# Modulation chunks mixed into the weight streams in pairs, and two of layer 1's modulation rounds moved later

## Chip, core and metric

One NeuronCore of a Trainium2 chip runs the whole kernel. The metric is the device time of one execution in microseconds. Of the kernel before, three executions were timed: 2155.64, 2166.26 and 2171.59 us, median 2166.26 us.

## What is computed

Two transformer layers run over 256 latent tokens and 256 context tokens, 1024 features wide, in float32:

```python
for l in range(DEPTH):                                   # 2 layers
    mod_l = cond_lat @ ada_w[l] + ada_b[l]               # 6 rows of 1024 from silu(c)
    mod_c = cond_ctx @ ada_w[l] + ada_b[l]
    sh1, sc1, g1, sh2, sc2, g2 = jnp.split(mod_l, 6, axis=-1)
    ...
    o_lat, o_ctx = token_mixer(modulate(x, sh1, sc1), modulate(xc, csh1, csc1), lp, rope, need_ctx)
    x = post_norm(alpha * x + g1 * o_lat, ln1_g[l], ln1_b[l])
    ...
    f_lat = swiglu(modulate(x, sh2, sc2), ...)           # layer 0; layer 1: moe_swiglu, top 2 of 8 experts
    x = post_norm(alpha * x + g2 * f_lat, ln2_g[l], ln2_b[l])
```

`token_mixer` is attention, an RWKV-7 scan and a Hyena convolution side by side, then one output projection. Layer 0 does all of it for both streams; in layer 1 the context is only read by the latent tokens.

The change concerns the modulation, `cond @ ada_w[l]`. A round makes two of the six rows: round 0 makes sh1 and sc1, round 1 g1 and sh2, round 2 sc2 and g2. So the first norm of a layer needs round 0, the residual norm after the mixer needs g1 of round 1, and the channel mixer needs rounds 1 and 2.

## The kernel before

All weights come from HBM in chunks of 512 KB ([128, 1024] float32), most of them issued on SP's DMA queue (tile `wraw`). `wload` loads a chunk and splits it into a rounded part and a rest: a cast on ScalarE (`whi`, L315) and a subtraction on VectorE (`wlo`, L316). Every product is then three passes on TensorE (`mm3`, L321 to L323). The number of buffers for raw chunks and for split pairs goes by the stage, `BUFS`: 6 raw and 4 pairs in stage "l" (both streams of layer 0, layer 1's context), 5 and 4 in stage "n" (layer 1's latent tokens), 30 and 4 in stage "m" (the experts).

The modulation is not split. `ada` (a generator) loads one chunk of `adaw` into a raw buffer of the stage's own ring and multiplies it as it is, in four matmuls that use a quarter of the array's columns each (tile `ada`, L392; the trace has two records for each of the four). Sixteen chunks make a round. After the last one VectorE adds the bias (L397), for rounds 1 and 2 two small stores put the rows into DRAM (`drow`), four transposes (`adaT`, L404) and copies put them feature-major into `modT`. The rows that are needed on all partitions are read back from `drow` by `modbc` (L420): `gate` in `post_norm`, `m_sc`, `m_sh` and `gate` in `moe_route`.

A generator in `s.fill` is mixed into the weight stream: each `wload` runs one step of it, which is one chunk of modulation:

```python
        if s.fill:
            next(s.fill, None)
```

Layer 0's rounds 1 and 2 are mixed into its first two mixers this way. All three rounds of layer 1 (48 chunks) are mixed into layer 0's channel mixer of the context, whose 66 weight chunks are products `ab` (L321 to L323, 24 matmuls with 256 columns to a chunk) and `fo` (12 matmuls with 512 columns).

After that come layer 0's channel mixer of the latent tokens, layer 1's context, and layer 1's latent part: `win` (input projection, tile `u`), `rwkv`, `attend` (`aS`, `aPT`, `ao`), the last four Hyena tiles of `win`, `hyena` (`Xc`, `Xs`, `hz`, `ho`) and `w_out` (tile `wo`, eight weight chunks), with its residual norm on VectorE (`pnr`, `x`). `moe_route` then picks the experts, and `moe_pass` streams 528 chunks of expert weights.

The program's order is not the order on an engine: the framework places instructions of independent parts between each other on each engine's queue. The queues are then run strictly in that order, and each instruction waits for what it needs.

Of the kernel before, what the change touches and what calls it, by code (L numbers as in the profile page):

```python
# [5 lines left out]
D = 1024  # L6
L = 256
# [8 lines left out]
def feature_tiles():  # L16
    """Columns of w_in per 128-wide tile, -1 for padding."""
    t = []
# [44 lines left out]
NLAST = 512  # of the first group, kept throughout  # L63
# [8 lines left out]
def constants():  # L72
# [11 lines left out]
    # x -> (-x1, x0) on pairs: out[m] = sum_k perm[k, m] x[k]  # L84
# [14 lines left out]
    ang = np.concatenate([row[:, None] * inv, col[:, None] * inv], -1).astype(np.float64)  # [L, 32]  # L99
# [6 lines left out]
    S = np.sin(th)  # [t, k]  # L106
    S[:, 0] = (-1.0) ** k  # column k = 0 holds the Nyquist term
    put("C", C.reshape(2, 128, 256).transpose(1, 0, 2))
    # forward: lhsT [t, k]; inverse: lhsT [k, t] -> S transposed
# [17 lines left out]
    a, b = (p % 32)[:, None], np.arange(32)[None]  # row s, column t  # L127
    # per direction: (A, B, -A, B) masks; A strict, B inclusive
# [3 lines left out]
    # token order: ltri[p, tt, q] = 1 where token tt*128+p precedes q within the tile  # L132
# [5 lines left out]
    # within a chunk, from its first (second) half to the other one  # L138
# [5 lines left out]
def layout(i):  # L144
    """Device arrays from the inputs: layout only."""
    g = lambda n: np.asarray(i[n])
    A = {}
# [7 lines left out]
    aw = g("ada_w").reshape(2, 8, 128, 3, 4, 2, 256)  # l, k, p, r, j, h, n  # L155
    A["adaw"] = np.ascontiguousarray(aw.transpose(0, 3, 5, 1, 2, 4, 6))  # l, r, h, k, p, j, n
# [12 lines left out]
    A["win"] = np.ascontiguousarray(wp.reshape(2, 8, 128, 20, 128).transpose(0, 3, 2, 1, 4))  # l, tile, p, k, 128  # L169
    wo = g("w_out")[:, mix_rows()]  # L170
    A["wout"] = np.ascontiguousarray(wo.reshape(2, 4, 2, 128, 2, 512).transpose(0, 4, 1, 3, 2, 5))  # l, half, kh, p, k, n

    def w13(w1, w3):  # [..., 1024, 2816] -> [..., 11, kh, p, k, (w1 256 | w3 256)]
        e = w1.shape[0]
        u = np.stack([w1, w3], 1).reshape(e, 2, 4, 2, 128, 11, 256)  # e, m, kh, k, p, b, n
        return np.ascontiguousarray(u.transpose(0, 5, 2, 4, 3, 1, 6)).reshape(e, 11, 4, 128, 2, 512)

    def w2(w):  # [e, 2816, 1024] -> [e, half, 22, p, 512]
        e = w.shape[0]
        u = w.reshape(e, 11, 2, 128, 2, 512)  # L180
        return np.ascontiguousarray(u.transpose(0, 4, 1, 3, 2, 5))  # e, half, 11, p, 2, 512
# [6 lines left out]
    A["rows"] = np.stack([g("ln1_g"), g("ln1_b"), g("ln2_g"), g("ln2_b")], 1)  # l, 4, 1024  # L188
    pr = np.zeros((2, 128, NPRM), np.float32)

    def pp(name, a, col=0, r0=0):  # a: [2, rows]
        pr[:, r0:r0 + a.shape[1], PRM[name] + col] = a

    mu = g("rwkv_mu")  # [2, 2, 864]
# [64 lines left out]
class Trunk:  # L259
# [4 lines left out]
    def lasting(s, n):  # L264
        """n words per partition that are kept throughout."""
        assert s.used + n <= NLAST + s.SMALL
        s.used += n
        return s.keep[:, s.used - n:s.used]

    def k(s, shape, name, dt=F32):  # L270
        """A tile. All of the pool's are of 4 KB per partition: up to 1 (2) KB, four (two) of a name share
        one; up to 512 bytes, the slots of a small lasting ring are used in turn."""
# [24 lines left out]
    def fresh(s, *names):  # L297
        """The next small tiles of these names do not share one with the past ones."""
# [14 lines left out]
    def split(s, src, hi, lo, eng="a"):  # L313
        """hi + lo == src; both fit a float32r pass exactly."""
# [3 lines left out]
    def mm3(s, out, a, b, start, stop, **kw):  # L318
        """out += a.T @ b from (hi, lo) pairs: three float32r passes."""
# [5 lines left out]
    def rsqrt(s, x, n, eps, name):  # L325
        """x[:, :n] -> 1 / sqrt(x + eps): an estimate from the exponent, then Newton steps to float32."""
# [10 lines left out]
    def raw(s, src):  # L337
        """The next 4 KB per partition of the weight stream."""
# [4 lines left out]
        if s.w == "m" and s.loads % 16 == 0:  # some through another queue  # L343
# [6 lines left out]
    def wload(s, src):  # L350
        """A weight chunk (4 KB per partition) as an exact (hi, lo) pair."""
# [5 lines left out]
        if s.fill:  # L357
            next(s.fill, None)
        return hi, lo

    def drain(s):
        """The rest of the loads mixed into the weight stream."""
# [4 lines left out]
    def order(s, inst, first):  # L367
        """inst is not to be issued before first."""
# [3 lines left out]
    def behind(s):  # L372
        """Loads not to be issued before the last weight load so far."""
        return s.tc.issue_after(s.last.ins) if s.last is not None else contextlib.nullcontext()

# [1 line left out]
    def ada(s, l, rounds):  # L377
        """Rounds of two of the six rows of the modulation, in steps of one weight chunk."""
# [38 lines left out]
    def modbc(s, l, st, prm, name):  # L417
        """Row prm of a stream's modulation on all partitions: a [128, 1024] tile."""
# [6 lines left out]
    def ln_stats(s, src):  # L425
        """src: list of [128, 1024] -> (mean list, rstd list)."""
# [16 lines left out]
    def hT(s, l, st, prm, src, f32=None):  # L443
        """LN(src) * (1 + scale) + shift, feature-major, split: eight (hi, lo) pairs [128, 256]."""
# [24 lines left out]
    def win_steps(s, l, tiles, g):  # L469
        """u^T tiles of w_in from g["h"], each to its consumer."""  # L470
# [14 lines left out]
    def conv3(s, u, out, cp, cc, cn, bias):  # L485
        """out[t] = cp * u[t-1] + cc * u[t] + cn * u[t+1] + bias over the 256 tokens."""
# [9 lines left out]
class Mix(Trunk):  # L496
# [1 line left out]
    def sin_of(s, ps, f, fb, out):  # L498
        """out = sin(f * ps + fb), the argument reduced to [-pi, pi]."""
# [15 lines left out]
    def spec_load(s, l):  # L515
        """Filter parameters of a layer; the larger ones by a second call."""
# [1227 lines left out]
```

## Time and profile before

| | |
|---|---|
| timed executions | 2155.64, 2166.26, 2171.59 us |
| span of the profiled execution (first to last instruction) | 2151.5 us |
| median less this span | 14.8 us |
| TensorE busy | 2061.4 us (96%) |
| VectorE busy | 1650.1 us (77%) |
| ScalarE busy | 1117.6 us (52%) |
| moved by DMA | 469.15 MB, 218 GB/s on average |

The profiled execution's own time is given by its span only; what lies around the span (launch, end) is not in the trace, so the 14.8 us hold that and the spread of the executions. A TensorE that is busy is not a TensorE at its peak, since the ends of matmuls are modelled; the starts are measured. Shares over the whole span mix stages with different limits, so the rows below are by stage. The granted clock of TensorE is 1.00 at 2.4 GHz and 0.50 at 1.2 GHz.

### The profile page before, as it was taken

To read this page: it belongs to the slowest core of one execution; us is meant where nothing else is said; L and a number is where in the kernel's file an instruction comes from. 1 tells how busy PE (TensorE), PEld (TensorE's weight loads), DVE (VectorE), ACT (ScalarE), POOL (GpSimd) and SP (SyncE) were. 2 spreads that over 40 slices of the span, in tenths; PEclk is the share of its full clock that TensorE was granted. 3 is DMA by queue.
4 is the path that set the end of the run, shared out by engine and by line. 5 is a ranking of instruction groups with operands and counts; after the bars stand their busy time and mean duration, and the time that the engine had idled before them with its cause. 6 is when DMAs were issued, how large, how long until landed. Compare 5 with 4: busy or idle time off the path is not lost. (4 is left out here: it accounts for less than half of the span.)

```text
span 2151.5 us, 35770 instructions
## 1 busy us (share of the span) xinstructions
PE 2061.4 (96%) x13674; PEld 1684.2 (78%) x13674; DVE 1650.1 (77%) x3026; ACT 1117.6 (52%) x1639; POOL 111.3 (5%) x87
## 2 busy tenths in 40 slices
PE   8999999999999999989798998999999999999996
PEld 2878777678878898887487777788888888888885
DVE  6897777459754685776887448799899989998997
ACT  3532544242332344443244232787787877778773
POOL 0012001100000000010111100000000000000000
PEclk9999999999999999999899978899999999999998
DMA  8522332336686545323211018699999999999992
GB/s 292 191 74 98 138 129 90 114 115 230 247 335 244 196 177 196 138 88 113 104 60 33 31 56 335 218 319 362 363 334 368 354 344 350 361 358 345 360 356 107
DMA packets 147852, 469.15 MB, mean 218 GB/s; under 512 B 31636, under 2 KB 33972, under 8 KB 147672
## 3 DMA queue, kind: packets, MB, share of 16 engines
q1 hardware_dynamic: 123512, 446.27, 56.8%
q0 software_dynamic: 4816, 17.36, 2.2%
q10 hardware_dynamic: 19344, 3.15, 0.8%
q8 instruction: 109, 1.79, 0.3%
q14 instruction: 71, 0.58, 0.1%
HBM read 464.56 MB, written 2.16 MB: 217 GB/s over the span
## 5 line engine op out<-in xcount | busy, mean ns | idle before, releaser
L316 DVE TENSOR_TENSOR wlo<-wraw,whi 128x1024 fp32r<-128x1024 f32 x748 | 888.0, 1222 | 96.2 <-ACT whi L315 61.7
L315 ACT CAST whi<-wraw 128x1024 fp32r<-128x1024 f32 x748 | 751.7, 1049 | 143.6 <-DMA wraw<-in_fw_dram 40.6
L321 PE MATMUL ab<-whi,m_x 128*128 128x512 f32 x704 | 281.6, 400 | 0.0
L323 PE MATMUL ab<-whi,m_x 128*128 128x512 f32 x704 | 275.6, 391 | 0.0
L322 PE MATMUL ab<-wlo,m_x 128*128 128x512 f32 x704 | 275.0, 391 | 0.0
L321 PE MATMUL ab<-hp,whi 128*128 128x256 f32 x704 | 204.8, 292 | 2.6 <-ACT hp L315 2.0
L323 PE MATMUL ab<-hp,wlo 128*128 128x256 f32 x704 | 201.7, 287 | 1.8 <-DVE wlo L316 1.8
L322 PE MATMUL ab<-hp,whi 128*128 128x256 f32 x704 | 201.7, 287 | 1.3 <-DVE hp L316 1.1
L323 PEld LDWEIGHTS ab<-whi,m_x 128*128 128x128 f32 x704 | 132.1, 188 | 28.3
L321 PE MATMUL u<-hp,whi 128*128 128x256 f32 x512 | 150.2, 297 | 4.1 <-ACT hp L315 3.0
L322 PEld LDWEIGHTS ab<-wlo,m_x 128*128 128x128 f32 x704 | 132.5, 188 | 25.5 <-DVE wlo L316 0.2
L321 PEld LDWEIGHTS ab<-whi,m_x 128*128 128x128 f32 x704 | 132.2, 188 | 25.1
L321 PEld LDWEIGHTS ab<-hp,whi 128*128 128x128 f32 x704 | 135.9, 194 | 18.3 <-issue 11.0
L323 PE MATMUL u<-hp,wlo 128*128 128x256 f32 x512 | 147.9, 291 | 1.2 <-DVE wlo L316 1.1
L322 PE MATMUL u<-hp,whi 128*128 128x256 f32 x512 | 148.1, 292 | 0.0
L323 PEld LDWEIGHTS ab<-hp,wlo 128*128 128x128 f32 x704 | 136.1, 194 | 5.3 <-DVE wlo L316 2.9
L322 PEld LDWEIGHTS ab<-hp,whi 128*128 128x128 f32 x704 | 136.5, 194 | 2.1 <-DVE hp L316 2.0
L321 PE MATMUL mo<-whi,ffg 128*128 128x512 f32 x352 | 137.8, 392 | 0.0
L323 PE MATMUL mo<-whi,ffg 128*128 128x512 f32 x352 | 137.1, 390 | 0.0
L322 PE MATMUL mo<-wlo,ffg 128*128 128x512 f32 x352 | 137.0, 389 | 0.0
L957 POOL TENSOR_TENSOR rBD<-rAT,cst 128x1024 f32<-128x1024 f32 x28 | 67.5, 2418 | 932.8 <-DVE rTm L995 509.9
L321 PEld LDWEIGHTS u<-hp,whi 128*128 128x128 f32 x512 | 98.4, 194 | 15.9 <-issue 6.5
(395 smaller groups left out, 3610.3 us busy)
## 6 DMA issues: line engine op xcount, KB each, us to landing
wraw<-in_mw_dram SPq DMA_DIRECT2D x495, 512.0 KB, 5.6
wraw<-in_fw_dram SPq DMA_DIRECT2D x132, 512.0 KB, 5.2
wraw<-in_adaw_dram SPq DMA_DIRECT2D x96, 512.0 KB, 5.1
wraw<-in_win_dram SPq DMA_DIRECT2D x64, 512.0 KB, 5.7
wraw<-in_mw_dram POOLq DMA_DIRECT2D x33, 512.0 KB, 6.8
wraw<-in_wout_dram SPq DMA_DIRECT2D x24, 512.0 KB, 3.6
lngb<-in_rows_dram SPq DMA_DIRECT2D x12, 512.0 KB, 6.3
x<-in_xs_dram SPq DMA_DIRECT2D x8, 512.0 KB, 6.0
```

Of the source, the lines that this page charges most:

```text
L315: i = (s.nc.scalar.copy if eng == "a" else s.nc.vector.tensor_copy)(hi, src)
L316: return i, s.nc.vector.tensor_sub(lo, src, hi.bitcast(F32))
L321: mm(out, a[0], b[0], start=start, stop=False, **kw)
L322: mm(out, a[0], b[1], start=False, stop=False, **kw)
L323: mm(out, a[1], b[0], start=False, stop=stop, **kw)
L957: i = nc.gpsimd.tensor_mul(x.rearrange("p u (j t) -> p u j t", j=4), bc(ATu[:, :, m, None, :], [128, 8, 4, 32]), bc(mask.rearrange("p (j t ...
```

## The change

`wload` now runs the generator at every second call only, `rate` steps at a time. `rate` is 2 from the start and 4 in layer 1's `w_out`. `turn` counts on over the whole kernel while a generator stands in `fill`. Of layer 1's three rounds only round 0 stays in the context's channel mixer. Round 1 is a loop of its own between layer 1's attention and the last four Hyena tiles of `win`, and round 2 is mixed into `w_out`, four chunks at every second of its eight weight chunks. Comments were removed as well, which moves line numbers by 3 or 4.

```diff
@@ wload
         s.cut = s.split(raw, hi, lo)
         if s.fill:
-            next(s.fill, None)
+            s.turn += 1
+            if s.turn % 2 == 0:
+                for _ in range(s.rate):
+                    next(s.fill, None)
         return hi, lo
@@ setup
         s.rings, s.packs, s.loads = {}, {}, 0
+        s.turn, s.rate = 0, 2
@@ body
-        s.fill = s.ada(1, [0, 1, 2])
+        s.fill = s.ada(1, [0])
         xc = s.whole(f)
         s.drain()
...
         s.win(1, ATT + HY[:2], gl)
         s.go(s.attend(1, gl, oT))
+        for _ in s.ada(1, [1]):
+            pass
         s.win(1, HY[2:], gl)
         s.go(s.hyena(1, gl, oT))
+        s.fill, s.rate = s.ada(1, [2]), 4
         x = s.w_out(1, LAT, oT, x)
+        s.drain()
         s.w = "m"
         s.moe(1, x)
```

The first place is SP's queue from layer 1's last input tiles to the experts' first weights. `wraw<-in_win` are chunks of the input projection, `in_adaw` of the modulation, `in_wout` of the output projection, `in_mw` of the experts; `drow` are the stores and reads of the modulation rows. Before:

```order
L347 DMA wraw<-in_win_dram 128x1024 x15
L347 DMA wraw<-in_wout_dram 128x1024 x8
L420 DMA m_sc<-drow 128x1024
L1380 DMA rout<-in_rout_dram 128x64
L347 DMA wraw<-in_mw_dram 128x1024 x4
L420 DMA gate<-drow 128x1024
L1198 DMA lngb<-in_rows_dram 128x1024 x2
L420 DMA m_sh<-drow 128x1024
L347 DMA wraw<-in_mw_dram 128x1024 x28
```

And now, first the input projection with round 1, then the end of `w_out` with the end of round 2 (between the two pieces the rest of round 2 stands among the other `wout` chunks):

```order
L347 DMA wraw<-in_win_dram 128x1024 x11
L388 DMA ada<-in_adab_dram 128x512
L347 DMA wraw<-in_adaw_dram 128x1024 x16
L347 DMA wraw<-in_win_dram 128x1024 x4
L347 DMA wraw<-in_wout_dram 128x1024
L347 DMA wraw<-in_adaw_dram 128x1024 x4
```

```order
L347 DMA wraw<-in_wout_dram 128x1024
L423 DMA gate<-drow 128x1024
L1201 DMA lngb<-in_rows_dram 128x1024
L404 DMA drow<-ada 4x512
L1383 DMA rout<-in_rout_dram 128x64
L347 DMA wraw<-in_mw_dram 128x1024
L423 DMA m_sc<-drow 128x1024
L1201 DMA lngb<-in_rows_dram 128x1024
L347 DMA wraw<-in_mw_dram 128x1024 x3
L423 DMA m_sh<-drow 128x1024
```

Sixteen modulation chunks now stand ahead of the last four input chunks, sixteen more stand among the `wout` chunks, and the experts' first chunks stand behind a store of round 2's rows, so behind round 2's end.

The second place is TensorE's queue where round 1 went, between the end of attention (`ao`, `aPT`) and the input projection (`u`). Before:

```order
L1181 MATMUL ryT<-keep,rvt 128x128 x4
L780 MATMUL aPT<-keep,aP 128x128 x4
L770 MATMUL aS<-akv,aq 128x512
L784 MATMUL ao<-aPT,akv 64x128 x4
L780 MATMUL aPT<-keep,aP 128x128 x4
L321 MATMUL u<-hp,whi 128x256
```

And now, from the third of these rows on:

```order
L787 MATMUL ao<-aPT,akv 64x128 x3
L783 MATMUL aPT<-keep,aP 128x128 x4
L395 MATMUL ada<-wraw,keep 32x256 x5
L787 MATMUL ao<-aPT,akv 64x128 x4
L783 MATMUL aPT<-keep,aP 128x128 x4
L395 MATMUL ada<-wraw,keep 32x256 x8
```

Round 1's 64 matmuls stand in 11 groups from here to the first `u`, with the rest of attention and the first half of Hyena between them; `u` no longer stands among attention's last products.

The third place is VectorE's queue in the residual norm after `w_out`, ahead of the row that makes the first half of the new `x` (`x<-x,keep,lngb`). Before:

```order
L1252 SCALAR_TENSOR_TENSOR x<-pnr,keep,lngb 128x1024
L334 SCALAR_TENSOR_TENSOR keep<-keep 128x1
L330 TENSOR_SCALAR keep<-keep 128x1
L332 TENSOR_TENSOR keep<-keep 128x1 x2
L333 SCALAR_TENSOR_TENSOR keep<-keep 128x1 x2
L334 SCALAR_TENSOR_TENSOR keep<-keep 128x1 x2
L1254 SCALAR_TENSOR_TENSOR x<-x,keep,lngb 128x1024
```

And now:

```order
L332 TENSOR_TENSOR keep<-keep 128x1 x2
L316 TENSOR_TENSOR wlo<-wraw,whi 128x1024
L333 SCALAR_TENSOR_TENSOR keep<-keep 128x1 x2
L316 TENSOR_TENSOR wlo<-wraw,whi 128x1024
L334 SCALAR_TENSOR_TENSOR keep<-keep 128x1 x2
L316 TENSOR_TENSOR wlo<-wraw,whi 128x1024
L1257 SCALAR_TENSOR_TENSOR x<-x,keep,lngb 128x1024
L332 TENSOR_TENSOR keep<-keep 128x1
L316 TENSOR_TENSOR wlo<-wraw,whi 128x1024
```

The splits of the experts' first four chunks, and the row `m_sc<-m_sc` a little ahead of this piece, have moved from `w_out` into the residual norm.

## Rows read from the trace of the kernel before

**Rows 1.** The page: span, and granted TensorE clock in 40 equal slices.

```profile
span 2151.5 us, 35770 instructions
...
PEclk9999999999999999999899978899999999999998
```

**Rows 2.** Stages: start:end, length, busy us (instructions) of PE, PEld, DVE, ACT, POOL, clock, DMA share, GB/s.

```profile
435.00:445.00 10.00, 10.00 (x54) 6.42 (x52) 2.66 (x5) 1.87 (x4) 0.00 (x0) 0.52 0.16 53
445.00:455.00 10.00, 10.00 (x54) 5.95 (x55) 6.70 (x25) 5.23 (x13) 0.00 (x0) 0.96 0.02 4
...
520.00:696.00 176.00, 175.63 (x1396) 140.54 (x1395) 102.58 (x172) 59.84 (x72) 0.00 (x0) 1.00 0.77 278
...
1245.00:1270.00 25.00, 23.65 (x79) 14.57 (x77) 10.80 (x35) 7.72 (x18) 0.00 (x0) 0.50 0.00 0
1270.00:1290.00 20.00, 20.00 (x154) 18.82 (x154) 8.05 (x15) 10.37 (x18) 0.58 (x1) 0.96 0.39 134
1290.00:1324.00 34.00, 34.00 (x156) 28.67 (x154) 25.76 (x49) 8.81 (x10) 0.00 (x0) 1.00 0.81 312
1324.00:1357.00 33.00, 21.76 (x108) 20.96 (x107) 26.82 (x90) 9.01 (x14) 0.54 (x1) 0.54 0.75 284
...
1450.00:2050.00 600.00, 600.00 (x2767) 496.06 (x2766) 551.16 (x607) 464.36 (x584) 13.18 (x25) 1.00 0.96 355
```

**Rows 3.** Timeline of TensorE: start, length, line, operation, count.

```profile
443.03 1.93 PE L392 MATMUL ada<-wraw,keep 128*32 128x256 f32 x14
...
603.14 0.64 PE L392 MATMUL ada<-wraw,keep 128*32 128x256 f32 x8
603.71 0.38 PE L321 MATMUL ab<-hp,whi 128*128 128x256 f32 x1
...
604.17 0.28 PE L321 MATMUL ab<-hp,whi 128*128 128x256 f32 x1
...
604.53 0.28 PE L321 MATMUL ab<-hp,whi 128*128 128x256 f32 x1
...
606.78 0.64 PE L392 MATMUL ada<-wraw,keep 128*32 128x256 f32 x8
```

**Rows 4.** The tile `ada` from 520 to 696 us: durations, first and last start.

```profile
L392 PE MATMUL ada<-wraw,keep x384: 379/379/403, 520.7 to 694.7; 128*32 128x256 f32 x192
```

**Rows 5.** Waits of TensorE's matmuls, 1170 to 1324 us: total us, times, longest.

```profile
PE ao L784 <- ACT aPT L782: 1.5, 3, 0.7
```

**Rows 6.** Timeline of SP's DMA issues: first start, time to the last, count.

```profile
1144.07 138.54 SPq L347 DMA_DIRECT2D wraw<-in_wout_dram  x8
1282.71 0.39 SPq L420 DMA_DIRECT2D m_sc<-drow  x1
...
1283.71 2.46 SPq L347 DMA_DIRECT2D wraw<-in_mw_dram  x4
...
1303.99 40.11 SPq L347 DMA_DIRECT2D wraw<-in_mw_dram  x28
```

**Rows 7.** DMA issues of the page: count, KB each, median us to landing.

```profile
wraw<-in_adaw_dram SPq DMA_DIRECT2D x96, 512.0 KB, 5.1
...
gate<-drow SPq DMA_DIRECT2D x6, 512.0 KB, 7.1
...
rD<-rTm ACTq DMA_DIRECT2D x16, 32.0 KB, 1.8
```

**Rows 8.** Costliest groups of the page: the two splits; count, busy us, mean ns.

```profile
L316 DVE TENSOR_TENSOR wlo<-wraw,whi 128x1024 fp32r<-128x1024 f32 x748 | 888.0, 1222 | 96.2 <-ACT whi L315 61.7
L315 ACT CAST whi<-wraw 128x1024 fp32r<-128x1024 f32 x748 | 751.7, 1049 | 143.6 <-DMA wraw<-in_fw_dram 40.6
```

**Rows 9.** Timeline of VectorE around the end of `w_out`.

```profile
1295.11 0.69 DVE L1381 TENSOR_SCALAR m_sc<-m_sc 128x1024 f32<-128x1024 f32 x1
...
1331.35 1.28 DVE L1254 SCALAR_TENSOR_TENSOR x<-x,keep,lngb 128x1024 f32<-128x1024 f32 x1
```

**Rows 10.** Waits in the experts' part, 1450 to 2050 us.

```profile
ACT whi L315 <- DMA wraw<-in_mw_dram: 0.3, 1, 0.3
```

## Prediction

> **What bounds the kernel now.** I read the page first: a span of 2151.5 us in which TensorE has its full clock nearly everywhere, with dips in slices 21 to 25 [rows 1]. So I asked by stage which engine is full where the change takes work out and where it puts it in. In the context's channel mixer (520 to 696 us) TensorE is busy 175.63 of 176 us at the full clock, VectorE 102.58, and DMA is at 0.77 [rows 2]. There a modulation chunk costs TensorE's time and no transfer. In the latent part of layer 1 (1270 to 1324 us) TensorE is busy 20.00 of 20 and 34.00 of 34 us [rows 2], and from 1170 to 1324 us the largest wait of its matmuls for another engine sums to 1.5 us [rows 5]. DMA is at 0.39 and 0.81, so this stage has room on the DMA and none on TensorE. Behind `w_out`, from 1324 to 1357 us, VectorE is the full engine (26.82 of 33 us) while TensorE idles a third of the time at the half clock [rows 2]: residual norm and routing are one chain of small VectorE steps, and what is put into VectorE's queue there is paid in full. In the experts' part TensorE is busy 600.00 of 600 us [rows 2] and the casts waited 0.3 us in total for weights [rows 10], so it starts when routing ends and then takes its own time.
>
> **What a chunk costs on TensorE.** Among the products `ab` one chunk starts at 603.14 us, the next at 606.78: 3.64 us for 24 products and a chunk. Three products without one take 604.53 - 604.17 = 0.36 us, so 24 take 2.88 and the chunk 0.76. From the chunk's start to the first product behind it are 0.57 us; the other 0.19 is the change of kind, paid once for a group [rows 3]. A chunk that stands right behind another therefore costs 0.57.
>
> **The sum, against the span of 2151.5 us.**
>
> Removed from the context's mixer: the tile `ada` has 384 records from 520 to 696 us [rows 4], eight to a chunk, so 48 chunks. 32 of them leave: 32 x 0.76 = 24.3 us less. Nothing else there takes the time back, since VectorE has 73 us free and DMA load falls. The 16 that stay come in pairs, which saves at most 8 x 0.19 = 1.5 us and nothing where the queue had them side by side already; I take 1.
>
> Layer 0's own 32 chunks also come in pairs: at most 16 x 0.19 = 3.0 us, at least nothing, because parts of that mixer are not full on TensorE. I take 2. The framework also reorders these products around them, for which I allow 3 either way.
>
> Added in layer 1: TensorE's queue has round 1 in 11 groups and round 2 in 10. That is 32 x 0.57 + 21 x 0.19 = 22.2 us. The first three chunks run where the clock is 0.50 [rows 2] and cost twice their body, some 1 us beyond what other work there would have paid; so 23. No idle time of TensorE covers it, as said. The transposes and stores of two rounds move with them, and the bias adds go to a VectorE that has room.
>
> Waits that this adds in layer 1: on SP's queue 16 modulation chunks now precede the last four input chunks, and the ring has five buffers, so the first input chunk is issued only when round 1's twelfth chunk has been used. It lands after 5.1 us [rows 7], is cast in 1.05 and split in 1.22 [rows 8], 7.4 us in all. TensorE has four chunks, the transposes of `adaT` and a little of Hyena for that time, some 4 us, and then waits about 3 us; behind it in its queue stand all four `u` tiles. In `w_out` 24 chunks pass the same five buffers. At 28 chunks in 40.11 us [rows 6] they need 1.43 us each, 34 us, beside about 33 us of products: nearly even. Half of the first chunks are there in time, so I take 1 us, between 0 and 8. Together 4 us, bounds 0 and 11.
>
> The residual norm behind `w_out`: before, the experts' first four chunks and `m_sc` were issued from 1282.71 us [rows 6], 40 us ahead of the end of `w_out`, and `m_sc` was worked on at 1295.11 us [rows 9], under `w_out`'s products. Now these steps stand in the chain: four splits of 1.22 [rows 8] and one of 0.69 us [rows 9], 5.6 us. They may also come late. SP first waits for the store of round 2's rows. Fifteen `wo` products stand behind the last modulation chunk; at 600 us for 2767 products [rows 2] that is 3.3 us before the end of `w_out`. Then come the bias add and the store. No row has the landing of so small a store; the nearest is 1.8 us for 32 KB [rows 7]. So `m_sc` is issued about 0.5 us before the end and lands, as `gate` does, 7.1 us later [rows 7], at +6.6. VectorE would want it about 3 us ahead of the row that stood at 1331.35 us (+7.35) [rows 9], at +4.4. The experts' chunks behind it come at 1.43 us each, and the third split ends near +13. I take 8 us for the whole; below stands 5.6 (nothing late), above 14 (`gate` of the residual norm, now read behind the last `wout` chunk, late by another 7.1).
>
> Sum: -24.3 - 1 - 2 + 23 + 4 + 8 = +7.7 us, a span of 2159. The median of the runs lies 14.8 us above the profiled span, so I add the change to the median: 2174 us. The moved rounds buy on TensorE about what they cost again, and the new order pays at the end of `w_out`.
>
> **Rivals.**
>
> *The latent part has slack that the busy time hides.* Ends of matmuls are modelled, so 34.00 of 34 us could hold gaps, and DMA does have room there. Then the moved chunks would be nearly free: -24.3 - 1 - 2 + 0 + 0 + 8 = -19 us, 2147. The Trainium skill ("Trainium Kernel Development and Optimization", section Performance Expectations) says that matmul busy time is a bad measure of how close a kernel is to its limit, because matmuls are pipelined; by that rule this rival would be the likelier one. Against it: the waits are read from starts and releases, and they are small [rows 5]; the same density is found in the context's mixer, where the starts are 0.12 us apart without a hole [rows 3]. Half hidden, it gives 2162, no measurable change.
>
> *The clock.* This one ends on the slower side. From 1245 to 1270 us TensorE was busy 23.65 of 25 us and yet had the half clock [rows 2]; it came back once the dense `u` products began, and these now come behind round 1. In `w_out` TensorE waits more often for chunks. With 54 us of old and 23 of new work from 1270 us on, a third of it at 1.2 GHz costs 26 us more: 2200. The point from which it decides is a granted clock under about 0.8 over this stretch. The Trainium skill ("TensorE: Matmul & The Clock Gate", section HAM oscillation) describes this pattern: bursts of matmuls between waits for DMA fall back to the half clock each time. Against it: in layer 0's attention the clock was 0.52 from 435 to 445 us and 0.96 in the ten after [rows 2], and just there stand 14 records of modulation, at 443.03 us [rows 3]; so this work seems to lift the clock, not to lower it. The waits I expect are of 3 us and less.
>
> *The experts starve.* Their loads begin some 40 us later against the end of `w_out`, so instead of 34 chunks about 26 are there when the first product starts. If the eight missing ones were paid at 1.43 us each, 11 us more: 2186. Against it: they are used at 355 GB/s [rows 2], one in 1.48 us, and were loaded one in 1.43 us [rows 6], so the store of chunks does not run dry.
>
> *The change does nothing that can be seen.* The pairs change little, and the chain at the end hides its splits in VectorE's 6 us of idle time [rows 2]: 24 out, 23 in, 2166.
>
> **How the numbers follow.** Forecast 0.60 (2160 to 2188), slack in the latent part 0.13, clock 0.14, starving 0.05, no effect 0.08. The predicted time is the forecast's, 2174 us. A measurement of this kernel can tell about 1% from no change, 21.7 us, so faster means under 2144.6 and slower over 2187.9. Faster: somewhat under half of the slack rival, 0.05. Slower: the clock rival and the upper tails of forecast and starving, 0.19. Same: 0.76. The range runs from 2150 (slack rival, most of it) to 2194 (the forecast with its upper bounds of waits and norm partly met, and the milder part of the clock rival); what it leaves out is 0.05 below and 0.13 above.
>
> **What would show it.** In the changed kernel's profile: the context's mixer from its first to its last product 24 to 26 us shorter, TensorE still full there; each moved chunk 0.57 us or more between products in `w_out`; a wait of TensorE on `whi` or `wlo` ahead of the first `u` behind round 1, of 2 to 4 us; from the first matmul of round 1 to the end of `w_out` some 25 us more than the same work before; VectorE from the last `wo` to the first expert product 6 to 10 us longer, with `wlo` in it and a wait for `m_sc`; the experts' pace unchanged. I am wrong if the stretch to the end of `w_out` grows by less than 15 us (slack), if its clock falls under 0.8 (clock), if the casts of the experts wait for DMA beyond a few us (starving), or if layer 0 moves by more than 5 us.

## The result

| | before | after |
|---|---|---|
| median of 20 timed executions each | 2159.80 us | 2182.86 us |
| lowest and highest | 2152.01, 2178.76 us | 2165.97, 2201.02 us |
| ratio, with 95% interval | | 1.0093 (1.0070 to 1.0116) |
| span of the profiled execution | 2151.5 us | 2177.4 us |
| mean granted clock in it | 0.967 | 0.951 |

The change costs some 20 us, 0.9%. That is within the 1% called no change, by a hair (the interval excludes zero and reaches over the 1%), and inside the range of the prediction, 9 us above its number. A second set of runs of the changed kernel gave 1.0084 (1.0050 to 1.0118). The comparisons, and the mean times at the half clock below, leave out executions more than 1.5% above the fastest of their kernel, and since these are executions with much time at the half clock it lowers such a mean: from 194 to 177 us for the kernel with pairs in layer 0 alone (three of twelve left out) and from 178 to 172 us for before on one chip (six of 35).

The page after, in answer to [rows 1]: the span, and the granted clock in 40 slices.

```profile
span 2177.4 us, 35693 instructions
...
PEclk9999999699999999999889598899999999999998
```

New are the 6 in the eighth slice (layer 0's recurrence and attention of the latent tokens) and the 5 in the 23rd (layer 1's recurrence and attention), where before has a 9 there and a 7 in the slice behind it. To see what each stage does, I cut both traces at the same events: first `u` of layer 0's latent part, first `wo`, first `ab`, a place in the context's channel mixer just behind the products that before mixes modulation into, the latent mixer's first `ab`, last `fo` of that mixer, last `u` of layer 1's first input tiles, end of the recurrence, last `u`, last `wo`, first product of the experts. Stages by windows, columns as in [rows 2], some left out. Before:

```profile
276.80:456.20 179.40, 172.67 (x1613) 130.64 (x1612) 109.99 (x311) 66.16 (x140) 23.15 (x12) 0.96 0.31 105
...
522.40:697.00 174.60, 174.23 (x1392) 140.50 (x1390) 101.25 (x168) 58.03 (x69) 0.00 (x0) 1.00 0.76 277
...
1156.40:1265.30 108.90, 105.85 (x807) 77.64 (x808) 52.78 (x165) 36.41 (x80) 14.13 (x8) 0.87 0.05 16
1265.30:1288.30 23.00, 23.00 (x160) 19.87 (x159) 11.17 (x23) 11.34 (x21) 0.58 (x1) 0.86 0.26 93
1288.30:1324.00 35.70, 35.70 (x163) 30.16 (x162) 26.57 (x51) 9.37 (x11) 0.00 (x0) 1.00 0.82 313
1324.00:1358.00 34.00, 22.76 (x116) 21.96 (x115) 26.82 (x90) 9.79 (x15) 0.54 (x1) 0.55 0.73 276
1358.00:2151.50 793.50, 774.10 (x3546) 636.39 (x3544) 717.93 (x807) 597.94 (x748) 16.34 (x31) 0.99 0.90 330
```

After:

```profile
272.70:467.00 194.30, 186.31 (x1619) 145.52 (x1618) 114.18 (x319) 67.01 (x142) 22.63 (x12) 0.86 0.29 99
...
533.20:680.00 146.80, 145.42 (x1127) 134.32 (x1125) 98.54 (x162) 57.43 (x70) 0.00 (x0) 1.00 0.67 225
...
1140.50:1258.30 117.80, 115.32 (x811) 83.94 (x812) 50.83 (x158) 34.77 (x80) 13.11 (x8) 0.80 0.01 2
1258.30:1300.00 41.70, 37.93 (x315) 27.24 (x316) 18.48 (x38) 11.97 (x20) 0.00 (x0) 0.96 0.80 272
1300.00:1342.50 42.50, 40.68 (x260) 26.54 (x259) 18.75 (x34) 8.60 (x10) 1.12 (x2) 1.00 0.79 285
1342.50:1383.90 41.40, 23.86 (x115) 22.99 (x116) 32.96 (x99) 13.87 (x19) 0.00 (x0) 0.59 0.80 299
1383.90:2177.40 793.50, 774.00 (x3546) 636.57 (x3544) 729.42 (x807) 612.89 (x748) 16.37 (x31) 0.99 0.92 338
```

The reader should see three things. The context's mixer is 27.8 us shorter up to the place where I cut it (28.6 us in all). The two stages with the moved rounds are 18.7 and 6.8 us longer and the way to the experts 7.4; the experts' 793.50 us are untouched. And two stages into which nothing was moved are longer: layer 0's latent part by 14.9 us at a clock of 0.86 in place of 0.96, and layer 1's attention and recurrence by 8.9 us at 0.80 in place of 0.87, with nearly the same count of instructions.

How much of that is one execution's luck, other traces tell. The changed kernel, profiled a second time, has 185.2 us at 0.92 in layer 0's latent part:

```profile
280.60:465.80 185.20, 175.58 (x1619) 136.78 (x1618) 116.15 (x319) 67.05 (x142) 22.58 (x12) 0.92 0.32 104
```

And the eight experiments below that have layer 0 in the order of before took 184.3 to 188.8 us there: the 179.4 us of before are the shortest of nine.

Still, in layer 0 one place can be named. The products `rN` of the recurrence all run ahead now, up to 379 us, and the serial state steps `rS` behind them have few other products between them. The windows around the first long run of them, and that run:

```profile
365.00:385.00 20.00, 18.43 (x183) 13.31 (x181) 12.61 (x36) 3.42 (x7) 5.88 (x3) 1.00 0.24 81
385.00:420.00 35.00, 34.29 (x201) 27.11 (x202) 12.18 (x47) 5.59 (x12) 3.39 (x2) 0.55 0.22 75
```

```profile
384.88 3.47 PE L1080 MATMUL rS<-rS,rMx 128*128 128x64 f32 x16 [1.57 <-DVE rS L1082]
```

TensorE waits 1.57 us for VectorE, runs sixteen steps, and the clock falls from 1.00 to 0.55 while it counts as busy 34.29 of 35 us.

The ends of the waits in the stretch of the moved rounds, 1259 to 1342 us, in answer to [rows 5] (engine, line, releaser: total us, times, longest):

```profile
PE ada L395 <- DMA wraw<-in_adaw_dram: 1.8, 2, 1.1
PE wo L322 <- DVE wlo L316: 1.8, 2, 1.2
PE adaT L407 <- DVE ada L400: 0.8, 1, 0.8
PE u L323 <- DVE wlo L316: 0.8, 1, 0.8
PE u L321 <- ACT whi L315: 0.4, 1, 0.4
```

Together 5.6 us, the same as the idle time that the two windows show (41.70 - 37.93 and 42.50 - 40.68).

Behind `w_out`, SP's issues and VectorE's timeline answer to [rows 6, 9] (start, length, line, operation, and the idle time ahead):

```profile
1337.53 0.49 SPq L404 DMA_DIRECT2D drow<-ada  x1
...
1341.23 0.33 SPq L423 DMA_DIRECT2D m_sc<-drow  x1
```

```profile
1347.81 0.68 DVE L1384 TENSOR_SCALAR m_sc<-m_sc 128x1024 f32<-128x1024 f32 x1
...
1353.32 0.17 DVE L1396 COPY keep<-m_lc 128x16 f32<-128x16 f32 x1 [2.23 <-PE m_lc L1393]
...
1353.55 1.22 DVE L316 TENSOR_TENSOR wlo<-wraw,whi 128x1024 fp32r<-128x1024 f32 x1
...
1354.82 1.22 DVE L316 TENSOR_TENSOR wlo<-wraw,whi 128x1024 fp32r<-128x1024 f32 x1
...
1356.10 1.22 DVE L316 TENSOR_TENSOR wlo<-wraw,whi 128x1024 fp32r<-128x1024 f32 x1
...
1357.23 1.28 DVE L1257 SCALAR_TENSOR_TENSOR x<-x,keep,lngb 128x1024 f32<-128x1024 f32 x1
```

The row that stood 7.35 us behind the end of `w_out` now stands 14.7 us behind it (1357.23 - 1342.5).

### The profile page after: what moved, and what is told of

Same layout as the page of the kernel before. It is cut to its first block, busy times and chain, and to the rows that moved or that the text cites. A ratio compares the mean times of both kernels' runs of the same rounds, so it can differ in the third digit from the quotient of the medians.

```text
span 2177.4 us, 35693 instructions
## 1 busy us (share of the span) xinstructions
PE 2074.0 (95%) x13674; PEld 1703.3 (78%) x13674; DVE 1662.2 (76%) x3026; ACT 1132.6 (52%) x1639; POOL 111.5 (5%) x87
## 5 line engine op out<-in xcount | busy, mean ns | idle before, releaser
L316 DVE TENSOR_TENSOR wlo<-wraw,whi 128x1024 fp32r<-128x1024 f32 x748 | 902.6, 1224 | 107.3 <-ACT whi L315 69.7
L315 ACT CAST whi<-wraw 128x1024 fp32r<-128x1024 f32 x748 | 771.3, 1052 | 293.2 <-PE ab L323 88.6
L323 PEld LDWEIGHTS ab<-whi,m_x 128*128 128x128 f32 x704 | 132.1, 188 | 28.6
L322 PEld LDWEIGHTS ab<-wlo,m_x 128*128 128x128 f32 x704 | 132.6, 188 | 25.3
```

Of the source, the lines that this page charges most:

```text
L315: i = (s.nc.scalar.copy if eng == "a" else s.nc.vector.tensor_copy)(hi, src)
L316: return i, s.nc.vector.tensor_sub(lo, src, hi.bitcast(F32))
L322: mm(out, a[0], b[1], start=False, stop=False, **kw)
L323: mm(out, a[1], b[0], start=False, stop=stop, **kw)
```

## A measure for the clock

Since the two traces differ most at the clock, I used what each timed execution lists, its span and mean granted clock: (1 - clock) x 2 x span is the time at 1.2 GHz, called the time at the half clock below. Within one kernel this moves a lot from execution to execution: for before, 170 to 173 us in the mean on three chips, with a spread (standard deviation) of 16 to 23 us. Over 237 executions of all kernels here, each against its own kernel's mean, an execution is 0.38 us longer for each us at the half clock; that alone takes the spread of the spans from 7.4 to 3.7 us. So a kernel's time has two parts: its mean time at the half clock, and the rest.

The changed kernel spends 210 us there (208 in the second set) against 172: 38 x 0.38 = 14 us. The means of the executions stand 17 to 20 us apart. So, by this estimate, some 3 to 6 us of the change are left for everything else that it does.

It also shows that the profiled execution of before was a fortunate one: its 0.967 means 142 us at the half clock, 30 less than that kernel's mean. By that alone, 11 us of the 26 between the two profiled spans belong to the draw; the profile of after (213 us) is an average one.

## The experiments

All start from the kernel before, with `wload` calling the generator by `if s.turn % s.every == 0: for _ in range(s.rate): next(s.fill, None)`. With `every` and `rate` 1 that is the kernel before. Ratios are against the kernel before on the same chip.

| kernel | ratio and interval | mean time at the half clock |
|---|---|---|
| changed kernel again | 1.0084 (1.0050 to 1.0118) | 208 us |
| pairs everywhere, no moves | 0.9987 (0.9955 to 1.0019) | 207 us |
| pairs everywhere, other phase | 1.0072 (1.0040 to 1.0105) | 217 us |
| pairs in layer 0 only | 0.9988 (0.9947 to 1.0029) | 177 us |
| pairs in the mixer only | 0.9985 (0.9950 to 1.0019) | 164 us |
| pairs in the mixer only, other phase | 0.9956 (0.9926 to 0.9986) | 172 us |
| fours in the mixer only | 0.9956 (0.9920 to 0.9993) | 178 us |
| both moves, no pairs | 1.0036 (1.0003 to 1.0068) | 188 us |
| round 1 moved | 1.0004 (0.9974 to 1.0034) | 183 us |
| round 2 moved | 1.0021 (0.9989 to 1.0053) | 162 us |
| both rounds ahead of `u` | 1.0111 (1.0073 to 1.0149) | 215 us |
| round 1 among the attention | 0.9968 (0.9939 to 0.9997) | 149 us |

### Pairs alone

```diff
-            next(s.fill, None)
+            # turn counts calls; every second call two steps
+        s.turn, s.every, s.rate = 0, 2, 2
```

> Pairs alone: every second weight load brings two modulation steps, and all three rounds of layer 1 stay in the context's channel mixer. Theory A (the pairing changes the order of layer 0's recurrent products, TensorE loses its full clock there): from the first `u` of layer 0's latent part to the first `ab` of the context's mixer 258 to 262 us instead of 245.6, with 40 us or more of that at the half clock instead of 14; the start some 4 us shorter; the context's mixer 1 to 5 us shorter; everything behind it as before. Whole kernel +6 to +12 us against before. Theory B (pairs cost nothing; the half clock in layer 0 was an accident of the one profiled execution): the stretch within 4 us of before, whole kernel -5 to +2 us.

Measured: 0.9987, which is -3 us (-10 to +4). Theory A's time fell, but its reason did not: the time at the half clock is 207 us against 172, worth 13 us, and yet the kernel is not slower. So the pairs would save some 16 us of work, more than either theory allowed; the trace shows half of it. The context's mixer, from its first `ab` to the first one of the latent mixer, took 220.8 us against 229.0. What a whole pair costs is seen below, in the run with the other phase.

The trace also gives a warning. Layer 0's latent part and layer 1's attention and recurrence of this kernel:

```profile
280.40:469.10 188.70, 178.53 (x1617) 139.54 (x1617) 113.49 (x319) 67.18 (x142) 22.57 (x12) 0.90 0.31 102
```

```profile
1159.20:1289.60 130.40, 127.36 (x809) 91.17 (x809) 53.15 (x165) 36.76 (x81) 14.12 (x8) 0.71 0.05 14
```

The second stage has the order of before, and took 130.4 us at 0.71 in place of 108.9 at 0.87. So one trace's clock in this stage is a draw, and the 8.9 us that the changed kernel's trace shows there prove nothing by themselves. All traces together say the same: seven with the order of before took 102.8 to 130.4 us in this stage, 116 in the mean, and five with round 1 behind the attention 114.4 to 117.9, 116 in the mean.

### Moves alone

```diff
-        s.fill = s.ada(1, [0, 1, 2])
+        s.fill = s.ada(1, [0])
@@ behind attend, and ahead of and behind w_out: as in the change
+        s.turn, s.every, s.rate = 0, 1, 1      # single steps until w_out
```

> Moves alone: single modulation steps per weight load in layer 0 and in the context's mixer, round 1 ahead of the last input tiles of layer 1's latent part and round 2 in `w_out` as in the change. Theory A: layer 0 as before within 2 us, context's mixer 24 to 25 us shorter, the stretch from the end of layer 1's recurrence to the end of `w_out` 24 to 27 us longer, the way to the first expert product 7 to 8 us longer; the attention and recurrence of layer 1's latent part either as before (then the whole is +7 to +9 us) or 10 us longer at the half clock, if the moved round reorders it (then +17 to +19 us). Theory B: all of the changed kernel's +20 us comes from the moves, +18 to +22 us.

Measured: 1.0036, +8 us (+1 to +15). Theory B, that the moves bring all of the 20 us, is outside the interval. By stages the context's mixer is 26.9 us shorter, the moved rounds' two stages 35.2 us longer (more than expected; 11.2 us of waits of TensorE stand in it, against 5.6 in the changed kernel), the way to the experts 7.6 longer. Layer 0's latent part, whose order is that of before, took 186.1 us against 179.4.

### Each round alone

```diff
-        s.fill = s.ada(1, [0, 1, 2])
+        s.fill = s.ada(1, [0, 2])              # round 1 alone: a loop behind attend
@@ the other kernel
+        s.fill = s.ada(1, [0, 1])              # round 2 alone: in w_out, four at a time
```

> Round 1 alone moved, single steps elsewhere, round 2 stays in the context's mixer. Theory A: context's mixer 12 us shorter; from the end of the recurrence to the end of `u` 17 to 18 us longer with round 1's 16 chunks in it; `w_out` and the way to the experts as before. Whole +5 us if layer 1's attention and recurrence stay as they were, +15 us if round 1 in the queue behind them brings them to the half clock (10 us). Theory B (the attention's 10 us have nothing to do with round 1): as before there, +5 us.

> Round 2 alone moved into `w_out`, single steps elsewhere, round 1 stays in the context's mixer. Context's mixer 12 us shorter, `w_out` 7 us (as between the two traces) to 12 us (16 chunks at 0.57 and 0.19 for each group) longer, the way from `w_out` to the first expert product 7 to 8 us longer because the experts' first splits and `m_sc` now stand in it. Whole +2 to +8 us. If the way to the experts stays as it was, the residual norm's part does not come from round 2's place, and the whole is -5 to 0 us. Layer 1's attention and recurrence as before by either theory.

Measured: 1.0004, +1 us (-6 to +7), and 1.0021, +5 us (-2 to +11). With round 1 moved, the context's mixer is 13.6 us shorter and the two stages to the end of `w_out` 17.2 longer; with round 2 moved 13.6 shorter and 12.4 longer. The way from the last `wo` to the experts' first product, first with round 1, then with round 2 moved:

```profile
1343.00:1377.80 34.80, 22.83 (x114) 22.03 (x114) 27.50 (x91) 9.79 (x15) 0.00 (x0) 0.56 0.87 333
```

```profile
1328.70:1370.50 41.80, 24.30 (x114) 23.38 (x115) 32.99 (x99) 13.78 (x19) 1.12 (x2) 0.55 0.91 335
```

The 7.8 us at the end come from round 2's place alone, and VectorE's busy time rises by the same 6 us as in the changed kernel (32.99 and 32.96 against 26.82 before).

### The changed kernel beside its parts

> The changed kernel again, beside the parts on one chip. From the four runs so far: within one kernel, an execution's time rises by about 0.41 us for each us that its TensorE spent at the half clock (mean clock and span of each execution), and kernels differ in that time: before 178 us in the mean, pairs alone 207, moves alone 188. Theory A (work and clock add up): work of the pairs -12, work of the moves +6, half clock about 210 us as with the pairs alone, +13: together +7 to +12 us, ratio 1.003 to 1.006. Theory B (the parts don't add up, the combination costs more): +18 to +22 us, ratio 1.008 to 1.010 as first measured.

Measured: 1.0084, +18 us (+11 to +26): theory B by its number, though the interval reaches down to theory A's +12. The parts' ratios add up to +5 us, and the whole is +18. With plain means of executions against the same runs of before the parts are +1.7 and +12.5 us and the whole +18.7. Whether 4 or 13 us are missing thus hangs on how runs of before are weighted, and the intervals of the parts are 14 us wide each; I can't call the difference shown.

### Pairs in one place

```diff
@@ mixer only
+        s.turn, s.every, s.rate = 0, 1, 1      # setup
+        s.turn, s.every, s.rate = 0, 2, 2      # ahead of the context's mixer
@@ layer 0 only
+        s.turn, s.every, s.rate = 0, 2, 2      # setup
+        s.every, s.rate = 1, 1                 # ahead of the context's mixer
```

> Pairs in the context's channel mixer only, all three rounds there, layer 0 and layer 1 in the order of before. Theory A (the pairs save work in the mixer and cost the clock in layer 0): mixer 7 to 9 us shorter, time at the half clock as before (178 us, within 10), the whole -5 to -10 us, ratio 0.9955 to 0.9975. Rival (the clock of pairs alone has nothing to do with layer 0's order): half clock 200 us or more, whole within 3 us of before.

> Pairs in layer 0 only, single steps in the context's mixer, nothing moved. Theory A (layer 0's changed order costs the clock): time at the half clock 200 to 215 us against 178 of before, worth +9 to +13 us, less 2 to 4 us of work saved: +5 to +11 us, ratio 1.002 to 1.005. Rival: half clock within 10 us of before and the whole -4 to +2 us.

Measured: 0.9985, -3 us (-11 to +4), and 0.9988, -3 us (-12 to +6). With pairs only in the mixer the clock is that of before, as theory A has it (164 us). With pairs only in layer 0 theory A expected 200 to 215 us at the half clock and found 177 (194 with all twelve executions). So the executions don't show that layer 0's new order alone costs what theory A put there, and with 177 or 194 they don't exclude it.

The traces do show that this order costs the clock at the place named above. In the kernel with pairs in layer 0 only, the same sixteen steps stand behind the same wait:

```profile
389.42 3.22 PE L1080 MATMUL rS<-rS,rMx 128*128 128x64 f32 x16 [1.57 <-DVE rS L1082]
```

From 385 to 420 us, first with pairs in layer 0 only, then in the mixer only:

```profile
385.00:420.00 35.00, 32.47 (x224) 25.68 (x223) 15.98 (x53) 5.59 (x12) 7.85 (x4) 0.72 0.20 68
385.00:420.00 35.00, 34.33 (x322) 24.78 (x322) 15.61 (x39) 10.00 (x21) 5.84 (x3) 1.00 0.31 106
```

All fourteen traces agree. From the first step `rS` of layer 0's latent part to the last, the five with pairs in layer 0 have 14 to 29 us at the half clock, and the nine with single steps there none. Over the whole latent part of layer 0 it is 31 to 58 us (47 in the mean) with pairs and 14 to 34 us (27) without; the part takes 191.5 us in the mean with them and 186.4 without.

The mixer gained less than expected, 3.6 us. TensorE's timeline shows where a part of it went: the queue cut four of the 24 pairs (sixteen records each), here into 10 and 6.

```profile
560.50 1.05 PE L395 MATMUL ada<-wraw,keep 128*32 128x256 f32 x10
561.48 0.39 PE L321 MATMUL ab<-hp,whi 128*128 128x256 f32 x1
...
564.54 0.63 PE L395 MATMUL ada<-wraw,keep 128*32 128x256 f32 x6
565.10 0.39 PE L321 MATMUL ab<-hp,whi 128*128 128x256 f32 x1
```

### The phase of the pairs

```diff
-        s.turn, s.every, s.rate = 0, 2, 2
+        s.turn, s.every, s.rate = 1, 2, 2      # everywhere; in the other kernel, in the mixer only
```

> As the pairs alone, but the pair comes with the first, third, fifth weight load instead of the second, fourth, sixth; the recurrent products of layer 0 again stand in another order. If pairs as such bring the half clock, 200 us or more of it and the whole within 4 us of before, as with the pairs alone. If it was only the order that the one phase happened to give, about 178 us of it and the whole -8 to -12 us, ratio 0.9945 to 0.9965.

> Pairs in the context's mixer only, as in the run before of this kind, but with the first, third, fifth weight load. In that run the queue split some pairs into 10 and 6 products and the mixer was 3.6 us shorter only; with this phase 23 pairs stay whole. If whole pairs give the gain, the mixer is 7 to 9 us shorter, the half clock 160 to 180 us as before, the whole -6 to -10 us, ratio 0.9955 to 0.997: faster than both kernels. If the phase means nothing, 3 to 4 us shorter and ratio 0.998 to 0.999.

Everywhere: 1.0072, +16 us (+9 to +23), which neither branch expected. The clock is as with the other phase (217 us), so pairs in both places bring the half clock whichever call they come with; and of the work they save in the context's mixer little is left, 2.1 us and not 8.2; this phase has the same pairs cut as the kernel with pairs in the mixer only. These 6 us and the 10 us more at the half clock don't account for all of the 19 us between the two phases; the rest stays open.

In the mixer only: 0.9956, -10 us (-16 to -3), with the context's mixer 8.2 us shorter, as expected of whole pairs. Here is one:

```profile
566.52 1.07 PE L395 MATMUL ada<-wraw,keep 128*32 128x256 f32 x16
567.52 0.39 PE L321 MATMUL ab<-hp,whi 128*128 128x256 f32 x1
```

From its start to the next product are 1.00 us. A lone chunk took 0.57 [rows 3], so the second costs 0.43 and a pair 1.00 + 0.19 against 2 x 0.76: 0.33 us saved, 24 times 8 us (22 of the 24 are whole). A pair cut as above takes 0.98 + 0.56 us and two changes of kind, 1.92 in all: more than two lone chunks. This kernel is faster than both that were given.

### Fours in the mixer

```diff
+        s.turn, s.every, s.rate = 0, 4, 4      # ahead of the context's mixer
```

> As the mixer's pairs, but four chunks with every fourth weight load. If a chunk behind a chunk costs 0.42 us and a lone one 0.77, twelve groups of four save 12 x 3 x 0.35 = 12.6 us; half the groups stay whole in the queue, so the mixer 7 to 12 us shorter, half clock as before, ratio 0.995 to 0.997. Rival: four modulation chunks take four of the six buffers of the weight ring and TensorE waits for `ab`'s weights: mixer shorter by less than 4 us or longer.

Measured: 0.9956, -10 us (-17 to -2), no better than whole pairs. The context's mixer is 5.7 us shorter, below the 7 to 12 expected and above the rival's 4: the queue keeps only some of the groups together. Its mean is 10 us under before's with the clock a little lower than before's (178 us).

### Both rounds ahead of the last input tiles

```diff
-        s.fill = s.ada(1, [0, 1, 2])
+        s.fill = s.ada(1, [0])
@@ behind attend
+        for _ in s.ada(1, [1, 2]):
+            pass
```

> Single steps as before, but rounds 1 and 2 both ahead of the last input tiles of layer 1's latent part, none in `w_out`. If the 7 to 8 us between `w_out` and the experts come from round 2's place (its late rows hold `m_sc` and the experts' first splits back), this stretch is 34 to 35 us again, as before and as with round 1 alone; if they come from having any round moved, it stays at 41 to 42. The 32 chunks in a row are limited by transfers at 1.43 us each, so from the end of the recurrence to the end of `w_out` some 35 to 45 us longer than before (with round 1 alone 17, with both places 25 to 35). Mixer 27 us shorter. Whole +5 to +15 us against before.

Measured: 1.0111, +24 us (+16 to +32), more than expected. The stretch from the end of the recurrence to the last `u`, the way to the experts, and the wait that rules the first:

```profile
1254.40:1335.80 81.40, 57.75 (x447) 32.84 (x448) 21.21 (x43) 13.75 (x23) 0.58 (x1) 0.73 0.67 232
1364.60:1398.90 34.30, 23.04 (x113) 22.25 (x114) 26.80 (x90) 9.85 (x16) 0.00 (x0) 0.55 0.82 309
```

```profile
PE ada L395 <- DMA wraw<-in_adaw_dram: 20.6, 16, 2.7
```

The way to the experts is 34.30 us again, 34.00 before, though both rounds are moved: the 7.4 us belong to round 2's place, and VectorE's busy time is back at 26.80. The first stretch is 58.4 us longer, and `w_out` 6.9 shorter: 51.5, where I had expected 35 to 45. Thirty-two chunks at 1.43 us would be 46 us; the trace has their products start between 1255.7 and 1316.8 us, one chunk in 1.97 us. TensorE waited 20.6 us for them, 2.7 at the longest, and with short bursts of modulation between these waits the clock was 0.73, so 2 x 0.27 x 81.4 = 44 us at the half level.

### Round 1 among the attention

```diff
-        s.go(s.attend(1, gl, oT))
-        for _ in s.ada(1, [1]):
-            pass
+        s.go(s.attend(1, gl, oT), s.ada(1, [1]))
```

(against the kernel with round 1 alone moved)

> As round 1 alone moved, but its chunks are taken in turn with the steps of layer 1's attention instead of behind them, so that dense products stand between the sparse ones. If such filler lifts the clock (as layer 0's attention before suggests), the attention and recurrence show under 30 us at the half clock instead of 48, and from the end of layer 1's first input tiles to the end of `w_out` the kernel is 8 to 20 us shorter than with round 1 behind the attention: ratio to before 0.993 to 0.998. If filler does nothing for the clock, 40 us or more at the half clock and a ratio of 0.999 to 1.003.

Measured: 0.9968, -7 us (-13 to -1), against +1 with round 1 behind the attention. Layer 1's attention and recurrence, first with round 1 behind them, then among them:

```profile
1149.40:1267.10 117.70, 115.23 (x812) 83.80 (x811) 50.88 (x157) 35.05 (x80) 13.10 (x8) 0.80 0.03 11
```

```profile
1147.90:1246.80 98.90, 97.78 (x851) 68.10 (x852) 46.75 (x149) 30.42 (x69) 13.18 (x8) 1.00 0.19 66
```

TensorE does 39 records more in 18.8 us less, at the full clock throughout. This is not only the draw of one trace: over twelve executions the time at the half clock is 149 us, against 183 with round 1 behind, and 34 x 0.38 = 13 us. No other of the fourteen traces has less than 13 us at the half clock in this stage. A second gain stands beside it: the 4.8 us that TensorE waited for round 1's chunks behind the attention are gone. So modulation products among the sparse products of the attention do lift the clock, as [rows 2, 3] had suggested of layer 0. The Trainium skill ("TensorE: Matmul & The Clock Gate", section HAM oscillation) advises, for thin matmuls in bursts with waits for DMA between them, to restructure the loop so that TensorE keeps its full clock. The stage here lost it otherwise: at 0.80, TensorE was busy 115.23 of 117.70 us and DMA stood at 0.03, so waits for DMA were not what had to be filled.

## Why the prediction was partly right

The forecast was +7.7 us and no change within 1%; the runs give +18 to +20 us, still just within it. That the time came out only 9 us above the forecast is in part luck: the forecast was added to a median of three executions, 2166.26 us, and the median of twenty is 2159.80; the change itself was missed by 10 to 12 us. Step by step:

**The context's mixer: right, and a little more.** 25.3 us were to leave, 27.8 did (28.6 to the mixer's end). The saving of a pair was mis-sized: I counted the second chunk at 0.57 us, as a lone one, and saw a gain only in the change of kind; it costs 0.43.

**The moved rounds: right in sum.** 23 us of TensorE's time and 4 of waits were expected, bounds 0 and 11 for the waits. The two stages are 18.7 + 6.8 = 25.5 us longer; busy time rose by 19.9 (37.93 + 40.68 - 23.00 - 35.70), waits are 5.6. TensorE's part was smaller, for grouped chunks cost less than I took; here is a run of four in `w_out`, 1.93 us in all:

```profile
1315.15 1.93 PE L395 MATMUL ada<-wraw,keep 128*32 128x256 f32 x32
```

The wait ahead of the first `u` behind round 1 was named as 2 to 4 us and is 1.2; that in `w_out` was taken as 1 and is 1.8; and 1.8 us of waiting for modulation chunks themselves were not in the list.

**The way to the experts: right in size, half right in its parts.** 8 us were forecast and 7.4 came; with both rounds early it was 34.30 us again. The splits and `m_sc` stand in the chain as said. But `m_sc` was not late: it was ready by 5.3 us behind the end of `w_out`, where I had it landing at 6.6. The fifteen products behind the last modulation chunk took 5.8 us and not 3.3, with a wait of 1.2 among them, so the store was issued 5 us ahead of the end. What filled its place is the wait of 2.23 us for `m_lc`, a product of the router's constants. They hang on round 2 as well: before, `m_lc` began with the end of `w_out` (1323.8 us), and now 7.2 us behind it (1349.7 us), and VectorE waits for it. Three splits (3.66), `m_sc` (0.68) and this wait make 6.6 of the 7.4 us by which the row at 1357.23 moved. The prediction had not followed that second reader of round 2.

**Slack in the latent part: wrong, as argued.** The stages grew by 25.5 us, far over the 15 that were to decide. (Half hidden, this rival's own terms give 2160.5 us, not 2162.)

**The experts starve: wrong, as argued.** 793.50 us before and after.

**The clock: the right cause at the wrong place.** The rival looked from 1270 us to the end of `w_out`, where the clock is 0.96 and 1.00, far above the 0.8 from which it was to decide. (The dips of before that the prediction read off [rows 1] stand in slices 20 and 24 to 26, not 21 to 25.) The cost came in stages that I had taken as fixed. I had set layer 0 at -2 us, with 3 either way for reordering, and named more than 5 us there as a sign of error; the two traces differ there by 10.8 (the start 4.1 shorter, the latent part 14.9 longer). Reordering was priced as products in another order at the same clock, and no term of the sum was for its effect on the clock. Over all executions the kernel spends 38 us more at the half clock, by the rate above some 14 of the 18 us.

**What is shown, and what stays open.** Shown by executions, not by one trace: the changed kernel and both kernels with pairs throughout spend 207 to 217 us at the half clock, the three with pairs in the mixer only 164 to 178, and before 170 to 173. (The kernel with both rounds early has 215 without any pairs; its trace has 44 of them in the stage with the waits.) Shown by the traces: with pairs in layer 0 the clock falls among the state steps of its recurrence, five times of five, and never in the nine kernels without. Shown as well: the moves without pairs cost 8 us (1 to 15), and round 2's place costs the way to the experts its 7 to 8 us.

Not shown is how the 38 us are spread over the stages, for the traces of a stage with one and the same order differ by as much. The means over the traces put some 20 us of it into layer 0's latent part and nothing into layer 1's attention. And it stays open how much of it pairs in layer 0 alone bring, 177 or 194 us against 170; more executions of that kernel, and several profiles of each, would tell.

**The run of before that I leaned on.** The sum was made against a profiled span of 2151.5 us, 14.8 us under the median shown. I carried that difference over as a constant. Most of it, some 11 us by the rate above, was the clock of one fortunate execution.

## What to carry to other kernels

Before reading a difference between two traces stage by stage, see how much of a kernel's time moves with its clock from execution to execution: two kernels are compared by their means, and a stage by its clock first. Small dense products were worth most among sparse ones here: the same sixteen chunks cost the kernel some 8 us less between the steps of the attention than behind it (13 us by the plain means, 2158.1 against 2171.1), and in groups of two they cost a fifth less each than alone, as long as the queue keeps the groups whole. When work is moved late, follow every reader of its result, not only the one that comes first.

## What the runs showed of the hardware

The same instructions in the same order got a clock of 0.71 in one profiled kernel and 0.93 in another, 130.4 against 102.9 us for 808 products; TensorE was busy 127.36 and 99.87 us of it. The row at 0.93:

```profile
1171.90:1274.80 102.90, 99.87 (x808) 73.26 (x809) 52.62 (x165) 36.96 (x81) 14.12 (x8) 0.93 0.10 33
```

The Trainium skill ("TensorE: Matmul & The Clock Gate", section What's actually happening) says that the number of matmuls at the half clock at a kernel's start varies from run to run, and puts this ramp under 1% of a typical span. That it varies agrees with these runs, in which the time at the half clock has a spread of 16 to 23 us between executions of before. But here the clock falls anew within the kernel, and one kernel's executions spread by 1.8% (2145.95 to 2183.80 us for before on one chip), most of which goes with the clock.

TensorE can count as busy and still lose its clock: with pairs in layer 0 it did so among the state steps there in five traces of five (in the changed kernel's, 0.55 for 35 us with 34.29 us busy).

A modulation chunk behind another costs 0.43 us and a lone one 0.57 plus 0.19: for these products, which use a quarter of the array's columns, the neighbours in the queue decide 43% of the time.
